# Low halves, a gate multiply and parts of the even mixer move from GpSimd to VectorE

## The chip, the cores and the metric

The kernel runs on one core of one Trainium2 chip. A core has five engines that each take their instructions in the order in which the program lists them: TensorE (PE in the profile, its weight loads PEld), VectorE (DVE), ScalarE (ACT), GpSimd (POOL) and SyncE (SP), which here only starts transfers between main memory and the core's own memories. The metric is the device time of one launch in microseconds, as the median of several runs.

## The reference, cut to what matters

One inference step of a small trunk with two layers. 128 context tokens and 512 latent tokens go through the same weights; the modulations (shift, scale, gate) come from a conditioning vector, one for the context and one for the latent tokens.

```python
for l in range(2):
    sh1, sc1, gt1, sh2, sc2, gt2 = ada_mod(c, w_ada[l], b_ada[l])
    h = rms_norm(x, g_mix_pre[l]) * (1 + sc1) + sh1
    y = even_mixer(h) if l == 0 else mla_mixer(h)   # each: h @ w_in ... @ w_out
    x = x + gt1 * rms_norm(y, g_mix_post[l])
    h = rms_norm(x, g_mlp_pre[l]) * (1 + sc2) + sh2
    y = square(relu(h @ w_mlp1[l])) @ w_mlp2[l]     # 1024 -> 4096 -> 1024
    x = x + gt2 * rms_norm(y, g_mlp_post[l])

# even_mixer: 4 heads of gated linear attention and 4 of retention, in both directions
#   o_gla = rms_norm(scan_f + scan_b, gla_norm) * silu(ga); o_ret = rms_norm(...) * silu(gb)
# mla_mixer: q, ckv, kpe = split(h @ w_in); 8 heads; keys and values from ckv @ w_kv_b
#   o = softmax(q k^T / sqrt(192)) v over 128 context, 128 cached and 512 latent keys
```

A context token attends to context tokens alone. All is float32.

## The kernel before

**Tiles and stages.** The 640 tokens are five tiles of 128 (t = 0 the context, 1 to 4 the latent tokens). The stages follow each other: the even mixer with its input projection, its output projection, the first MLP, the odd mixer (attention) with its input projection, its output projection, the second MLP. Beside them run the modulations of later stages (`rada`, `ada`), and all weights are loaded once, in the order of a list.

**Float32 by three products.** TensorE multiplies in a short format (fp32r). So each weight and each activation is kept as two halves, high = the cast, low = what the cast has lost, and `mm3` makes high x high, high x low and low x high. The cast is ScalarE's (`nc.scalar.copy`), the low half is a subtraction (`tensor_sub`), on GpSimd or VectorE by an argument `lo`. In the trace a weight's raw copy is `raw`, its halves are `wh` and `wl` (where both lie in one tile, `wp`), the activations' halves are `hT` (two constant tiles, the high one and the low one), and the float32 value ahead of it `h`.

**A weight's way.** `weights` (L409) starts a load as soon as one of three `raw` buffers is free; `weight_rooms` (L423) waits for the load and takes a place among ten `w` buffers; `weight_split` (L449) does the cast and the low half, gives `raw` back and announces the weight. `nat_units` (L462) does this for projections, in four parts of two contraction blocks each for each group of columns; the first group of the odd layer's projection is 256 wide (splits of 128x512), the second 320. `mlp_units` (L860) does it for the MLP in eight blocks: four weights of the first and four of the second product, each 128x1024. Before the change the low halves of both projections of each mixer, of the attention heads' weights, and of the first four weights of each MLP are GpSimd's; the other MLP weights are VectorE's.

**An activation's way.** `pre_norm` (L723) takes the square sum (ScalarE), a root by a few one-column instructions (`sm`), scales the tile (`y` or `xn`), has TensorE turn it in eight blocks (`ps`), modulates four of them on VectorE and four on ScalarE (`h`), and splits them (`hT`) in two halves of 128x512. Its low half is GpSimd's after the first tiles and after the MLP, and "either" after an output projection. The MLP's `tail` (L1033) runs for each token tile after the last block: it adds the last partial sum to `y` (VectorE), sums its squares (ScalarE), multiplies by the gate (GpSimd, L1046), then `residual` (L774) and the next `pre_norm`. The squared ReLU is `relu` (L1019): ScalarE's relu and square, GpSimd's square in float32, VectorE's difference.

**What sets the order.** The instructions are written by a list scheduler, `Weave` (L95). Each piece of work is a generator that hands instructions to engines and yields where the next one depends on the last. The planner keeps a clock for each engine, with a cost for each instruction from `Engine.way` (L267): VectorE 0.07 + n/960 us, GpSimd 0.2 + 0.00215 n, for n elements of a row. One more clock, "port", stands for the memory port that VectorE's two-input instructions and GpSimd's share. Among those that are ready at an engine's next free time it emits the one of the lowest priority number, on VectorE the one of the oldest thread, and so on. A weight's split has priority 1 (or 0 with `prio=0`), the token tiles' work 0 or below. With "either" the planner picks the engine that would end first. The result is one fixed list for each engine. At run time an engine takes its list in order, and an instruction whose input is not there holds up all behind it.

All instructions are issued from one line, `emit` (L269), so in the profile every row bears L269 and is known by its tiles. Here is the code that the change touches and what calls it.

## Time and profile before

| | |
|---|---|
| time, median of 3 runs | 1567.67 us (1564.66 to 1568.7) |
| profiled execution | 1567.55 us |
| its span in the trace | 1565.8 us |
| mean granted TensorE clock | 0.982 of full speed |
| read and written in main memory | 158.73 and 5.96 MB, 105 GB/s |

The span is what the trace covers; the profiled execution's time has 1.75 us more around it. The two-dimensional picture of the span (40 slices of 39 us, digits in tenths of busy time) shows how the engines share it:

```profile
PE   5999999999999999999998999989999999999997
DVE  4254755655777787777667688865675333334335
ACT  3583533645323223223245466654543222322322
POOL 1433744331012012102165110051202101211213
PEclk8999999999999999999997999999999999999999
```

GpSimd is busiest from 39 to 352 us (slices 2 to 9: the even mixer, its output projection and the first MLP's entry), from 783 to 861 us (slices 21 and 22: the odd layer's entry) and from 1018 to 1057 us (slice 27: the weights of the odd output projection). TensorE is below nine tenths in slices 1, 22, 27 and 40, and its granted clock below nine tenths in slices 1 and 22.

### The profile page before, as it was taken

How to read it: one execution, taken by the hardware profiler on the slowest of the kernel's cores; microseconds unless marked ns; L12 is line 12 of the kernel's file. 1: busy time of each engine (PE TensorE's matmuls, PEld its weight loads, DVE VectorE, ACT ScalarE, POOL GpSimd, SP SyncE). 2: the span in 40 equal slices, each digit the busy share in tenths (PEclk: the TensorE clock that was granted, in tenths of full speed). 3: DMA queues.
4: the chain of work that ended last, by engine and by line, in shares of the span. 5: the costliest groups of instructions: out<-in, count | busy, mean ns of one | idle time of the engine just before them, and what ended most of it. 6: DMA issues, size and time to landing. Idle time of an engine off the chain costs nothing.

```text
span 1565.8 us, 23013 instructions
## 1 busy us (share of the span) xinstructions
PE 1508.6 (96%) x8731; PEld 1338.3 (85%) x8731; DVE 939.7 (60%) x1776; ACT 635.0 (41%) x1467; POOL 387.3 (25%) x317
## 2 busy tenths in 40 slices
PE   5999999999999999999998999989999999999997
PEld 1687888888899889989977899978889988998996
DVE  4254755655777787777667688865675333334335
ACT  3583533645323223223245466654543222322322
POOL 1433744331012012102165110051202101211213
PEclk8999999999999999999997999999999999999999
DMA  9455322222554445444323001032353322222211
GB/s 333 150 180 182 87 73 62 93 85 92 182 159 139 140 139 146 142 133 128 99 85 120 14 21 28 28 97 72 102 173 103 88 76 74 81 72 67 77 54 67
DMA packets 146734, 166.19 MB, mean 106 GB/s; under 512 B 11984, under 2 KB 92480, under 8 KB 146624
## 3 DMA queue, kind: packets, MB, share of 16 engines
q1 hardware_dynamic: 146624, 164.73, 34.4%
q8 instruction: 68, 1.11, 0.3%
q14 instruction: 42, 0.34, 0.1%
HBM read 158.73 MB, written 5.96 MB: 105 GB/s over the span
## 4 chain that ended last, share of the span: by engine, by line
PE 89%; DVE 4%; ACT 3%; DMA 1%; issue 1%; POOL 1%; SPq 1%; DVEq 0%; ACTq 0%; POOLq 0%
PE p L269 56%; PE pg L269 18%; PE ps L269 12%; PE pqk L269 2%; DVE sm L269 1%; PE pv L269 1%; ACT junk L269 1%; DVE x L269 1%; DMA x<-in_x_sample 1%; DMA rada<-in_w_ada 1%; SPq L269 1%; DVE y L269 0%; DVE prob L269 0%; ACT h L269 0%; ACT wh L269 0%
## 5 line engine op out<-in xcount | busy, mean ns | idle before, releaser
L269 PE MATMUL p<-hT,wh 128*128 128x256 f32 (+1 forms) x2048 | 450.7, 311 | 4.8 <-ACT hT L269 4.2
L269 PE MATMUL p<-wh,hid 128*128 128x512 f32 x1280 | 398.7, 390 | 0.0
L269 PEld LDWEIGHTS p<-hT,wh 128*128 128x128 f32 x2048 | 347.4, 190 | 6.9 <-ACT hT L269 4.7
L269 PE MATMUL p<-hT,wl 128*128 128x256 f32 (+1 forms) x1024 | 317.8, 310 | 0.0
L269 POOL TENSOR_TENSOR r<-r 128x384 f32<-128x384 f32 (+1 forms) x128 | 132.6, 1036 | 729.5 <-ACT hid L269 700.5
L269 PEld LDWEIGHTS p<-wh,hid 128*128 128x128 f32 x1280 | 240.3, 188 | 49.6
L269 ACT CAST wh<-raw 128x1024 fp32r<-128x1024 f32 (+3 forms) x169 | 172.5, 1026 | 261.6 <-PE p L269 220.6
L269 PE MATMUL pg<-wh,hT 128*128 128x512 f32 (+3 forms) x840 | 265.6, 388 | 0.0
L269 PE MATMUL p<-wl,hid 128*128 128x512 f32 x640 | 249.6, 390 | 0.0
L269 DVE TENSOR_TENSOR wl<-raw,wh 128x1024 fp32r<-128x1024 f32 x121 | 148.1, 1224 | 107.5 <-ACT wh L269 107.3
L269 PEld LDWEIGHTS p<-hT,wl 128*128 128x128 f32 x1024 | 195.0, 190 | 0.0
L269 PEld LDWEIGHTS pg<-wh,hT 128*128 128x128 f32 x840 | 155.6, 191 | 29.4 <-issue 6.7
L269 ACT ACTIVATE r<-p 128x384 f32<-128x384 f32 (+1 forms) x128 | 56.1, 438 | 268.5 <-PE p L269 268.5
L269 DVE TENSOR_TENSOR y<-y,p 128x512 f32<-128x512 f32 x140 | 95.8, 685 | 103.5 <-PE p L269 103.2
L269 POOL TENSOR_TENSOR wl<-raw,wh 128x1024 fp32r<-128x1024 f32 (+3 forms) x44 | 100.1, 2290 | 217.5 <-ACT wh L269 106.8
L269 DVE SCALAR_TENSOR_TENSOR ada<-rada,cT,ada 128x512 f32<-128x512 f32 x196 | 146.8, 783 | 0.0
L269 DVE TENSOR_TENSOR hid<-r,hid 128x384 fp32r<-128x384 f32 (+1 forms) x128 | 63.6, 497 | 130.5 <-POOL r L269 130.5
L269 PE MATMUL pg<-wl,hT 128*128 128x512 f32 (+3 forms) x360 | 141.6, 393 | 0.0
L269 PEld LDWEIGHTS p<-wl,hid 128*128 128x128 f32 x640 | 120.2, 188 | 24.1
L269 PEld LDWEIGHTS pg<-wl,hT 128*128 128x128 f32 x360 | 68.6, 191 | 13.6 <-issue 4.4
L269 ACT ACTIVATE hid<-r 128x384 fp32r<-128x384 f32 (+1 forms) x128 | 60.4, 472 | 2.2
L269 POOL TENSOR_TENSOR wp<-raw,wp 128x512 fp32r<-128x512 f32 (+1 forms) x18 | 25.2, 1405 | 96.3 <-ACT wp L269 96.3
(257 smaller groups left out, 2006.2 us busy)
## 6 DMA issues: line engine op xcount, KB each, us to landing
raw<-in_w_mlp SPq DMA_DIRECT2D x128, 512.0 KB, 4.1
rada<-in_w_ada SPq DMA_DIRECT2D x160, 256.0 KB, 3.4
rada<-in_w_ada SPq DMA_DIRECT2D x16, 512.0 KB, 9.1
raw<-in_w_in_even SPq DMA_DIRECT2D x16, 512.0 KB, 3.8
x<-in_x_sample SPq DMA_DIRECT2D x8, 512.0 KB, 6.8
gate<-gate SPq DMA_DIRECT2D x8, 512.0 KB, 4.7
raw<-in_w_out_even SPq DMA_DIRECT2D x8, 512.0 KB, 3.7
raw<-in_w_out_odd SPq DMA_DIRECT2D x8, 512.0 KB, 3.8
```

The lines of the kernel that those rows point to most:

```text
L269: emit = lambda: real(*a, **k)
```

## The change

Every low half that GpSimd made becomes VectorE's: of the weights of both mixers' projections, of the attention heads, of the first block of each MLP, and of the activations (`hT`); after the output projections, where the planner chose, VectorE now makes it always. The MLP tail's multiply by the gate becomes VectorE's. In the even mixer three operations do: the sum of the two masked score halves (A + B), the gate's multiply by the norm's gain (ga), and the two decayed keys (`ks`). GpSimd keeps the squared ReLU, the fills, the backward states, its half of the rotation, and one state product of the context tile. The planner's costs are not changed; with other engines for these instructions it writes other lists.

```diff
--- before.py
+++ after.py
@@ -720,7 +720,7 @@
             self.drop(hp, hw)
 
 
-    def pre_norm(self, t, x, xn, sm, mods, ready, halves=None, lo="gpsimd"):
+    def pre_norm(self, t, x, xn, sm, mods, ready, halves=None):
 
 
         nc, w = self.nc, self.w
@@ -758,7 +758,7 @@
             k = slice(half * 4, half * 4 + 4)
             nc.scalar.copy(self.hT[0][:, t, k], h)
             yield
-            getattr(nc, lo).tensor_sub(self.hT[1][:, t, k], h, self.hT[0][:, t, k].bitcast(F32))
+            nc.vector.tensor_sub(self.hT[1][:, t, k], h, self.hT[0][:, t, k].bitcast(F32))
             self.drop(hh)
             w.set(evs[half])
             if halves:
@@ -828,16 +828,16 @@
 
         io = self.io
         self.wlist = []
-        self.u_in_even = self.nat_units(io["w_in_even"][0], EVEN_GROUPS, "gpsimd", prio=0)
+        self.u_in_even = self.nat_units(io["w_in_even"][0], EVEN_GROUPS, prio=0)
         self.loaded = Event()
         self.wlist.insert(2, self.loaded)
         self.even_rooms = [Event() for _ in range(4)]
-        self.u_out_even = (self.nat_units(io["w_out_even"][0], OUT_GROUPS[:1], "gpsimd")
-                           + self.nat_units(io["w_out_even"][0], OUT_GROUPS[1:], "gpsimd", rooms=self.even_rooms))
+        self.u_out_even = (self.nat_units(io["w_out_even"][0], OUT_GROUPS[:1])
+                           + self.nat_units(io["w_out_even"][0], OUT_GROUPS[1:], rooms=self.even_rooms))
         self.u_mlp = [self.mlp_units(0)]
         self.odd_rooms = [Event() for _ in range(4)]
-        self.u_in_odd = (self.nat_units(io["w_in_odd"][0], ODD_GROUPS[:1], "gpsimd", pair=True)
-                         + self.nat_units(io["w_in_odd"][0], ODD_GROUPS[1:], "gpsimd", rooms=self.odd_rooms))
+        self.u_in_odd = (self.nat_units(io["w_in_odd"][0], ODD_GROUPS[:1], pair=True)
+                         + self.nat_units(io["w_in_odd"][0], ODD_GROUPS[1:], rooms=self.odd_rooms))
         wq = io["w_q_b"][0].rearrange("(k p) (h c) -> p k h c", p=P, h=HC)
         wkv = io["w_kv_b"][0].rearrange("(k p) (h s c) -> p k h s c", p=P, h=HC, s=2)
         self.u_qpe = self.weight(lambda raw: [(raw[:, k], wq[:, k, :, 128:192]) for k in range(2)], [2, HC, 64])
@@ -846,15 +846,15 @@
         for h in range(HC):
             self.u_h.append(self.weight(lambda raw, h=h: [x for k in range(2) for x in (
                 (raw[:, k, 0], wq[:, k, h, 0:P]), (raw[:, k, 1], wkv[:, k, h, 0]))], [2, 2, P],
-                lo="gpsimd", pair=True, quota=quota))
+                pair=True, quota=quota))
             if h % 2 == 0:
                 self.u_v.append(self.weight(lambda raw, h=h: [(raw[:, k], wkv[:, k, h:h + 2, 1]) for k in range(2)],
-                                            [2, 2, P], lo="gpsimd", pair=True, quota=quota))
+                                            [2, 2, P], pair=True, quota=quota))
         self.heads_out = Event()
         self.wlist.append(self.heads_out)
         self.odd_out_rooms = [Event() for _ in range(4)]
-        self.u_out_odd = (self.nat_units(io["w_out_odd"][0], OUT_GROUPS[:1], "gpsimd")
-                          + self.nat_units(io["w_out_odd"][0], OUT_GROUPS[1:], "gpsimd", rooms=self.odd_out_rooms))
+        self.u_out_odd = (self.nat_units(io["w_out_odd"][0], OUT_GROUPS[:1])
+                          + self.nat_units(io["w_out_odd"][0], OUT_GROUPS[1:], rooms=self.odd_out_rooms))
         self.u_mlp.append(self.mlp_units(1))
 
     def mlp_units(self, l):
@@ -862,7 +862,7 @@
         w2 = self.io["w_mlp2"][l].rearrange("(f p) n -> p f n", p=P)
         res = []
         for b in range(FF // 512):
-            lo = "vector" if b else "gpsimd"
+            lo = "vector"
             prio = 0 if b else 1
             u1 = [self.weight(w1[:, :, fc * P:(fc + 1) * P], [KC, P], lo, prio=prio) for fc in range(b * 4, b * 4 + 4)]
             u2 = [[self.weight(w2[:, r0:r0 + 2, h * 512:h * 512 + 512], [2, 512], prio=prio)
@@ -978,7 +978,7 @@
             self.at_last(left, lambda: w.set(gfree))
             x = xs[t][0]
             yield from self.residual(x, y, sm)
-            yield from self.pre_norm(t, x, y, sm, mods, ready, None, "either")
+            yield from self.pre_norm(t, x, y, sm, mods, ready)
             self.drop(hy, hs)
 
         for t in range(NT):
@@ -1043,7 +1043,7 @@
                 yield
                 nc.scalar.activation(self.junk[:, 0:512], y[:, s], AF.Square, accum_out=sm[:, 4 + half:5 + half])
                 yield
-                nc.gpsimd.tensor_mul(y[:, s], y[:, s], gr[c][:, s])
+                nc.vector.tensor_mul(y[:, s], y[:, s], gr[c][:, s])
                 yield
             if gfree:
                 self.at_last(left, lambda: w.set(gfree))
@@ -1444,7 +1444,7 @@
                 nc.vector.copy_predicated(h4(M), masks[:, d].unsqueeze(1).broadcast_to((P, NH, P)), h4(pas[d][0]))
                 self.drop(pas[d][1])
                 yield
-            nc.gpsimd.tensor_add(A, A, B)
+            nc.vector.tensor_add(A, A, B)
             self.drop(hkt)
 
             v, hv = yield va
@@ -1459,7 +1459,7 @@
             ga, hga = yield from self.take(sg, [P, 512], F32, "ga")
             yield from silu_of(ps, hp, ga)
             yield
-            nc.gpsimd.tensor_mul(h4(ga), h4(ga), gn.unsqueeze(1).broadcast_to((P, NH, P)))
+            nc.vector.tensor_mul(h4(ga), h4(ga), gn.unsqueeze(1).broadcast_to((P, NH, P)))
             yield from mix_out(t, "gla", qt, v, pr, 1.0 / 64.0, 0.125, ga, ga)
             ya, hya = ga, hga
             self.drop(hqt, hv, hee)
@@ -1507,7 +1507,7 @@
             self.drop(hp)
             kv_ = k.rearrange("p (h c) -> p h c", h=NH)
             for d in range(2):
-                nc.gpsimd.tensor_mul(ks[:, :, d], kv_, kd[:, :, d].unsqueeze(2).broadcast_to((P, NH, 64)))
+                nc.vector.tensor_mul(ks[:, :, d], kv_, kd[:, :, d].unsqueeze(2).broadcast_to((P, NH, 64)))
             self.drop(hqk)
             yield
```

The numbers in the names below only count the tiles made, and differ between the two programs.

**The odd layer's entry.** Before, GpSimd's list stands as follows at the end of the first MLP. `y_3655` and `y_3657` are token tiles 3 and 4, `wp_7460` and `wp_7461` the third and fourth part of the projection's first weight group, `wp_7516` and the rest the second group.

```order
L269 TENSOR_TENSOR y_3655<-y_3655,gate_94 128x512
L269 TENSOR_TENSOR hT_92<-h_7420,hT_91 128x512
L269 TENSOR_TENSOR hT_92<-h_7422,hT_91 128x512
L269 TENSOR_TENSOR wp_7460<-raw_7221,wp_7460 128x512
L269 TENSOR_TENSOR wp_7461<-raw_7288,wp_7461 128x512
L269 TENSOR_TENSOR wp_7516<-raw_7300,wp_7516 128x640
L269 TENSOR_TENSOR y_3655<-y_3655,gate_94 128x512
L269 TENSOR_TENSOR y_3657<-y_3657,gate_94 128x512
L269 TENSOR_TENSOR hT_92<-h_7589,hT_91 128x512
L269 TENSOR_TENSOR hT_92<-h_7592,hT_91 128x512
L269 TENSOR_TENSOR wp_7553<-raw_7520,wp_7553 128x640
L269 TENSOR_TENSOR wh_7562<-raw_7554,wh_7561 128x640
```

The splits stand between the gate multiplies of tiles 3 and 4, and beside VectorE's own list. Now the same two parts are `wp_7478` and `wp_7479` in VectorE's list; `sm_3658` and `y_3657` belong to tile 4.

```order
L269 TENSOR_SCALAR sm_3658<-sm_3658 128x1
L269 TENSOR_SCALAR h_7649<-ps_7639,mod_4782,mod_4206 128x128 x2
L269 TENSOR_TENSOR wp_7478<-raw_7221,wp_7478 128x512
L269 SCALAR_TENSOR_TENSOR sm_3658<-sm_3658 128x1
L269 TENSOR_TENSOR hT_92<-h_7651,hT_91 128x512
L269 TENSOR_SCALAR sm_3658<-sm_3658 128x1
L269 TENSOR_TENSOR hT_92<-h_7649,hT_91 128x512
L269 TENSOR_TENSOR sm_3658<-sm_3658 128x1
L269 TENSOR_SCALAR y_3657<-x_3205,sm_3658 128x1024
L269 TENSOR_TENSOR wp_7479<-raw_7283,wp_7479 128x512
L269 TENSOR_SCALAR h_7696<-ps_7686,mod_4782,mod_4206 128x128 x4
```

The last addition of the MLP (the last partial sum onto tile 4) is 28 rows ahead of `wp_7478` and 35 ahead of `wp_7479`. So the two splits moved behind the gate multiplies, residuals and normalisations of the tiles before. On TensorE the first projection group of the first tile (`pg`) before runs through its four weight parts at once:

```order
L269 MATMUL pg_7525<-wp_7266,hT_91 128x256 x2
L269 MATMUL pg_7525<-wp_7266,hT_92 128x256
L269 MATMUL pg_7525<-wp_7460,hT_91 128x256 x2
L269 MATMUL pg_7525<-wp_7460,hT_92 128x256
L269 MATMUL pg_7525<-wp_7460,hT_91 128x256 x2
L269 MATMUL pg_7525<-wp_7460,hT_92 128x256
L269 MATMUL pg_7525<-wp_7461,hT_91 128x256 x2
L269 MATMUL pg_7525<-wp_7461,hT_92 128x256
L269 MATMUL pg_7525<-wp_7461,hT_91 128x256 x2
L269 MATMUL pg_7525<-wp_7461,hT_92 128x256
L269 MATMUL pg_7526<-wp_7516,hT_91 128x320 x2
```

Now the eight turns of tile 4 (`ps` with the identity) are put between the third part's products and the fourth's, which begin in the last two rows:

```order
L269 MATMUL pg_7562<-wp_7478,hT_91 128x256 x2
L269 MATMUL pg_7562<-wp_7478,hT_92 128x256
L269 MATMUL ps_7686<-ident,y_3657 128x128
L269 MATMUL ps_7687<-ident,y_3657 128x128
L269 MATMUL ps_7686<-ident,y_3657 128x128
L269 MATMUL ps_7687<-ident,y_3657 128x128
L269 MATMUL ps_7686<-ident,y_3657 128x128
L269 MATMUL ps_7687<-ident,y_3657 128x128
L269 MATMUL ps_7686<-ident,y_3657 128x128
L269 MATMUL ps_7687<-ident,y_3657 128x128
L269 MATMUL pg_7562<-wp_7479,hT_91 128x256 x2
L269 MATMUL pg_7562<-wp_7479,hT_92 128x256
```

What moved: the third part's products stand ahead of the turns of tile 4, the fourth part's behind them, and 241 TensorE instructions of this stage follow `wp_7479`'s.

**From softmax to the output projection.** VectorE before, at the last head's softmax: `prob` are the probabilities of a tile, `sm` their sums, `pt` the turned probabilities, each `sm` with its own number a tile.

```order
L269 TENSOR_TENSOR sm_10367<-sm_10367 128x1
L269 TENSOR_TENSOR sm_10399<-sm_10399 128x1
L269 RECIPROCAL sm_10367<-sm_10367 128x1
L269 TENSOR_TENSOR hT_92<-ps_10383,hT_91 128x128
L269 TENSOR_SCALAR prob_10366<-prob_10366,sm_10367 128x640
L269 RECIPROCAL sm_10399<-sm_10399 128x1
L269 TENSOR_TENSOR hT_92<-ps_10457,hT_91 128x2x128
L269 TENSOR_SCALAR prob_10398<-prob_10398,sm_10399 128x640
```

Between them GpSimd made the output projection's splits at the same time. VectorE now, at the same place:

```order
L269 TENSOR_SCALAR sm_10378<-sm_10378 128x1
L269 TENSOR_TENSOR wl_10261<-raw_9827,wh_10260 128x1024
L269 TENSOR_TENSOR wl_10419<-raw_10331,wh_10418 128x1024
L269 TENSOR_TENSOR sm_10378<-sm_10378 128x1
L269 RECIPROCAL sm_10378<-sm_10378 128x1
L269 TENSOR_SCALAR prob_10377<-prob_10377,sm_10378 128x640
L269 TENSOR_TENSOR wh_10421<-raw_10409,wh_10420 128x1024
L269 TENSOR_TENSOR pt_8256<-ps_10496,pt_8255 128x512
```

What moved: two splits (`wl`) stand between a tile's sum and its scaling of the probabilities, and a third behind the scaling.

## The prediction

> **What bounds the kernel now.** I read the page's busy line and chain first, then the windows, and last the timeline of the few stretches where TensorE waits.
>
> ```profile
> PE 1508.6 (96%) x8731; PEld 1338.3 (85%) x8731; DVE 939.7 (60%) x1776; ACT 635.0 (41%) x1467; POOL 387.3 (25%) x317
> PE 89%; DVE 4%; ACT 3%; DMA 1%; issue 1%; POOL 1%; SPq 1%; DVEq 0%; ACTq 0%; POOLq 0%
> ```
>
> TensorE (PE) is busy 1508.6 of 1565.8 us and makes 89% of the chain that ended last. GpSimd (POOL) has 387.3 us of work, but 1% of the chain. Relieving an engine that is 25% busy is worth nothing by itself; the change can win or lose only inside the 57 us (1565.8 - 1508.6) in which PE stands still, and in the slow clock that follows such pauses. The windows say where they lie:
>
> ```profile
> 20.00:30.00 10.00, 6.18 (x30) 2.76 (x28) 4.56 (x14) 5.36 (x11) 2.21 (x1) 0.69 1.05 394
> 30.00:40.00 10.00, 7.84 (x34) 3.95 (x31) 7.97 (x17) 4.50 (x9) 5.92 (x5) 0.63 1.05 391
> 200.00:300.00 100.00, 99.55 (x547) 83.46 (x546) 57.58 (x114) 44.10 (x81) 43.26 (x35) 1.00 0.18 54
> 820.00:830.00 10.00, 6.93 (x32) 6.56 (x32) 8.07 (x14) 5.74 (x18) 9.33 (x7) 0.66 0.36 110
> 840.00:850.00 10.00, 6.01 (x27) 5.12 (x26) 9.10 (x32) 6.04 (x17) 3.69 (x4) 0.51 0.24 87
> 900.00:1000.00 100.00, 98.32 (x737) 96.49 (x735) 81.73 (x251) 68.17 (x218) 9.88 (x8) 1.00 0.10 30
> 1030.00:1040.00 10.00, 6.25 (x39) 5.52 (x37) 6.90 (x19) 5.79 (x18) 3.68 (x2) 0.87 0.46 141
> ```
>
> Columns are the window, its length, busy us of PE, PEld, DVE, ACT, POOL, then granted clock, DMA share and GB/s. Between the pauses PE is full (99.55 of 100 us), so moving work there changes nothing unless the new owner falls behind. In the pauses VectorE (DVE) is the busy engine (9.10 of 10 us at 840), and the clock drops to 0.51 to 0.69. At first sight it is a bad moment to give DVE more work.
>
> **Why DVE looks fuller than it is.** Its rows while POOL works, and the same rows while POOL rests:
>
> ```profile
> 345.69 4.75 POOL L269 TENSOR_TENSOR wl<-raw,wh 128x1024 fp32r<-128x1024 f32 x2
> 345.98 2.12 DVE L269 TENSOR_TENSOR sm<-sm 128x1 f32<-128x1 f32 x1
> 348.20 3.33 DVE L269 SCALAR_TENSOR_TENSOR x<-y,sm,x 128x1024 f32<-128x1024 f32 x1
> 357.40 1.28 DVE L269 SCALAR_TENSOR_TENSOR x<-y,sm,x 128x1024 f32<-128x1024 f32 x1
> 1557.02 0.21 DVE L269 SCALAR_TENSOR_TENSOR sm<-sm 128x1 f32<-128x1 f32 x1
> 1557.46 0.16 DVE L269 TENSOR_TENSOR sm<-sm 128x1 f32<-128x1 f32 x1
> ```
>
> An instruction on one column takes 0.16 us alone and 2.12 us inside a GpSimd split; the residual takes 1.28 and 3.33. DVE is not computing for that long, it is held until GpSimd's instruction ends. So a part of DVE's busy time is waiting for POOL, and goes away with POOL's work.
>
> **What each moved instruction costs.**
>
> ```profile
> L269 POOL TENSOR_TENSOR wl<-raw,wh 128x1024 fp32r<-128x1024 f32 x32 | 79.5, 2506 | 166.5 <-ACT wh L269 86.2 <-DVE sm L269 34.6 <-PE ps L269 20.4
> L269 DVE TENSOR_TENSOR wl<-raw,wh 128x1024 fp32r<-128x1024 f32 x121 | 148.1, 1224 | 107.5 <-ACT wh L269 107.3
> L269 POOL TENSOR_TENSOR hT<-h,hT 128x512 fp32r<-128x512 f32 x20 | 27.8, 1403 | 12.2 <-ACT hT L269 11.1 <-DMA dist<-in_consts 1.1
> L269 DVE TENSOR_TENSOR hT<-h,hT 128x512 fp32r<-128x512 f32 x20 | 13.1, 689 | 3.9 <-ACT hT L269 3.8
> L269 DVE SCALAR_TENSOR_TENSOR sm<-sm 128x1 f32<-128x1 f32 x50 | 25.8, 524 | 13.0 <-ACT sm L269 13.0
> L269 DVE TENSOR_TENSOR sm<-sm 128x1 f32<-128x1 f32 x82 | 22.4, 279 | 5.8 <-ACT prob L269 4.4
> L269 DVE TENSOR_SCALAR h<-ps,mod,mod 128x128 f32<-128x128 f32 x80 | 28.8, 404 | 15.6 <-PE ps L269 15.2 <-POOL hT L269 0.2
> ```
>
> The same split takes 2506 ns on POOL and 1224 on DVE (ratio 0.49), the 512-wide form 1403 and 689. The gate multiply is of that 512-wide, two-input form, so I take 0.69 for it too. What stays on POOL is the squared ReLU, the fills, the backward states and half of the rotation, about 164 us; 223 move and become 0.49 x 223 = 110 us on DVE. Returned are at least 50 x (0.524 - 0.21) = 16 us and 82 x (0.279 - 0.16) = 10 us of holds on the statistics alone. DVE should end near 1010 us (65%), so in the mean it still has room. The sum goes place by place; negative is faster.
>
> **1. The start (20 to 40 us).**
>
> ```profile
> 24.97 2.21 POOL L269 TENSOR_TENSOR wl<-raw,wh 128x960 fp32r<-128x960 f32 x1 [24.53 <-DMA rada<-in_w_ada]
> 25.32 1.87 DVE L269 SCALAR_TENSOR_TENSOR sm<-sm 128x1 f32<-128x1 f32 x1
> 30.49 1.82 DVE L269 TENSOR_TENSOR sm<-sm 128x1 f32<-128x1 f32 x1
> 61.92 4.74 DMA rada<-in_w_ada
> ```
>
> The statistics of the second and third token tile are held for 1.87 - 0.21 and 1.82 - 0.16, 3.3 us on the path to the first projection. Now DVE makes the first split itself, ahead of that statistic (about 1.1 us, from 1.224 for a slightly wider one), and the second one behind the normalised tile, where it delays nothing. Left are about 2.2 us, and 0.7 from the activation's low half (1.40 to 0.69). A transfer stands in the chain at 61.92, so part may be hidden there. I take **-2.5**; ends 0 (the DMA ends it anyway) and -6 (all of PE's 6.0 idle us in these windows).
>
> **2. The two MLP entries (350 and 1100 us).** The splits of an MLP's first block hold the statistics and residual of token tile 2 by 2.12 - 0.16 and 3.33 - 1.28 us, and the first MLP matmuls wait for that tile:
>
> ```profile
> 361.04 0.45 PE L269 MATMUL p<-hT,wh 128*128 128x384 f32 x1 [2.10 <-ACT hT L269]
> ```
>
> 4.0 us of holds go; of the four splits (1.224 each) now on DVE three stand between this tile's instructions, but where DVE waited for ScalarE or PE anyway. I take **-2.5** for each entry, the wait and a little clock, **-5** together; ends +1 and -8 (a split that waits for its cast pushes the tile back, or both entries lose every wait).
>
> **3. The odd layer's entry (803 to 869 us): the place that decides.**
>
> ```profile
> 802.04 0.67 DVE L269 TENSOR_TENSOR y<-y,p 128x512 f32<-128x512 f32 x1
> 803.01 0.75 DVE L269 TENSOR_SCALAR y<-x,sm 128x1024 f32<-128x1024 f32 x1
> 812.46 5.47 POOL L269 TENSOR_TENSOR wp<-raw,wp 128x512 fp32r<-128x512 f32 x3
> 813.51:869.36 55.85, 45.21 (x297) 43.07 (x296) 39.56 (x113) 31.12 (x100) 28.46 (x22) 0.85 0.37 112
> 845.71:869.36 23.65, 23.65 (x169) 23.55 (x168) 14.23 (x52) 12.13 (x43) 6.81 (x7) 0.91 0.15 57
> ```
>
> PE ends the MLP at 813.5 and needs until 869.4 for 297 instructions, 10.6 us of it idle. In the new order DVE works through all five tiles first. The third and fourth low half of the projection's first weight group (wp_7478, wp_7479) stand 28 and 35 rows behind the last MLP addition, and PE's order puts 241 instructions behind wp_7479. From the second half of tile 2's addition (802.04 before) to the last addition the order holds some 12.6 us of free-running DVE work, so DVE gets there about when PE delivers, 814.5. From there to wp_7479 stand: fifteen small statistics (2.5 us), ten 512-wide passes with both splits (6.9), two residuals (2.6), three normalisations (0.75 each, 2.25), eight h pieces (0.40 each, the group of 80 above, 3.2) and an estimated 0.7 for two evictions: 18 us, less some 2.5 because consecutive instructions overlap. With 1.5 us for waits on ScalarE wp_7479 ends at 831.5. PE then has 241 instructions at 23.65 / 169 = 0.140 us: 33.7 us, end 865.2 against 869.4. I take **-3**; ends -8 (no waits, full clock) and +8 (DVE needs ten more us for the tiles). It breaks even if wp_7479 ends at 835.5.
>
> On the clock after such a pause, by the Trainium skill, page TensorE: Matmul & The Clock Gate, section What's actually happening, about 3.4 us without work halves the clock until about 3.4 us of work have passed. The windows at 820 and 840 agree with the direction (0.66, 0.51). By that rule one long wait before wp_7479 would cost an estimated 1.7 us more, and this term would be -1.3 instead of -3.
>
> **4. Attention (870 to 1020 us).** Twelve 512-wide splits move, 12 x 0.69 = 8.3 us onto a DVE that is 82% busy beside a PE at 98% (window at 900); the holds that go are of the same size. I take **0**, covered by DVE's spare 18%; without that cover the price is up to +5, and below nothing -2.
>
> **5. From softmax to the output projection (1030 to 1050 us).**
>
> ```profile
> 1033.34 0.54 DVE L269 TENSOR_SCALAR prob<-prob,sm 128x640 f32<-128x640 f32 x1
> 1035.14 2.34 POOL L269 TENSOR_TENSOR wl<-raw,wh 128x1024 fp32r<-128x1024 f32 x1 [3.79 <-ACT wh L269]
> 1035.30 2.53 DVE L269 TENSOR_SCALAR prob<-prob,sm 128x640 f32<-128x640 f32 x1
> 1037.97 1.94 PE L269 MATMUL ps<-ident,prob 128*128 128x128 f32 x8 [3.54 <-DVE sm L269]
> 1044.32 2.39 DVE L269 TENSOR_SCALAR prob<-prob,sm 128x640 f32<-128x640 f32 x1
> 1047.03 2.29 DVE L269 TENSOR_SCALAR prob<-prob,sm 128x640 f32<-128x640 f32 x1
> ```
>
> Scaling the probabilities takes 0.54 us free and 2.53, 2.39 and 2.29 beside a split: 5.6 us of holds in the last head's softmax, and PE waits 3.54 us behind the first. DVE now makes these splits; two stand ahead of the last tile's scaling (2.4 us). I take 5.6 - 2.4 = 3.2, and a little clock: **-3.5**; ends 0 and -6.
>
> **6. The end.**
>
> ```profile
> 1557.94 1.65 POOL L269 TENSOR_TENSOR y<-y,gate 128x512 f32<-128x512 f32 x1 [1.37 <-ACT junk L269]
> 1560.07 0.20 DVE L269 TENSOR_SCALAR sm<-sm 128x1 f32<-128x1 f32 x1
> ```
>
> The last gate multiply ends at 1559.6; on DVE it takes 0.69 from about 1557.8, and the statistic at 1560.07 can follow at 1558.55: **-1.5**; ends -1 and -2.
>
> **The even mixer** (weight splits, ga, qt, kr between 100 and 330 us) I cost at nothing: PE is full there by the window at 200 and DVE 58% busy. If DVE became the later one, every us is a us; I keep ends of 0 and +3. On SyncE's queue only constants, cache and parking transfers change places; earlier splits free the three raw buffers earlier, so no load moves behind its need.
>
> **Sum:** -2.5 - 5 - 3 + 0 - 3.5 - 1.5 = -15.5. The profiled execution took 1567.55 us, 0.1 below the median of 1567.67, so the forecast is **1552 us**.
>
> **Rivals.**
>
> *DVE becomes the bound at the odd entry (slower).* The splits are queued behind five tiles of residual and normalisation, where POOL made them beside DVE at 812.46. If the tiles take as long as now and wp_7479 comes only at an estimated 851, some 5 us past the 845.71 from which PE now runs unbroken, PE ends at 851 + 33.7 = 884.7, +15.3 instead of -3. If DVE is then the later engine in the attention stage too (+5), the total is 1552 + 18.3 + 5 = 1575. It turns slower than before once wp_7479 ends later than about 848. For it speaks DVE's 9.10 of 10 us at 840; against it, that much of this is held time.
>
> *Nothing net: 1566.* The waits of PE are refilled by others (the DMA at 61.92, ScalarE's casts, DVE's own splits), and only the end's 1.5 us stay. By the Trainium skill, page Perfetto Trace Analysis, section Optimizing Scalar/DVE Operations, moving operations between these two engines might not help, since they share a read port. That would be this rival, with the sum at 1566. The rows speak against it, since the same split holds the port 2.5 us from POOL and 1.2 from DVE.
>
> *Half: 1560.* The odd entry breaks even or loses 1 to 2 us, and the holds come back in part as DVE's own splits.
>
> *More: 1543.* The odd entry, the start and the entries reach their far ends, with the clock staying up.
>
> **How the numbers follow.** A measurement can tell about 0.3% (4.7 us) from no change. Forecast (1548 to 1557) 0.44, half 0.20, more 0.12, nothing net 0.13, slower 0.11. Faster by over 0.3% (below 1563): 0.44 + 0.20 + 0.12 = 0.76, less 0.02 of the half case that falls short of it, is 0.74. Same: 0.13, those 0.02 and 0.01 of the slower case, 0.16. Slower: the other 0.10. The range takes the forecast, the half case and most of the further gain, up to where nothing is left of it: 1542 to 1566.
>
> **What would show it.** POOL near 164 us, DVE near 1010; the statistics' two groups near 0.21 and 0.16 us each; no scaling of probabilities above 0.8 us; PE's idle time near 45 us or less; PE's wait at the odd entry as one block before wp_7479, ending by 833. Wrong would be a DVE row that waits for a cast with statistics behind it, idle time of PE in the even stage, or wp_7479 after 836.

## The result, and the profile after

The changed kernel takes 1542.75 us (median of 4 runs, 1541.48 to 1544.89) against 1567.95 us (1564.66 to 1568.7, 4 runs). The ratio is 0.9845, 95% interval 0.9827 to 0.9863: 25 us less, where 15.5 were forecast; the time lies 0.75 us above the lower end of the predicted range of 1542 to 1566. The profiled execution took 1542.66 us, its span is 1540.9.

From the page of the changed kernel, the busy line and the chain by engines:

```profile
PE 1495.1 (97%) x8731; PEld 1329.5 (86%) x8731; DVE 962.6 (62%) x1912; ACT 636.6 (41%) x1467; POOL 165.4 (11%) x181
PE 91%; DVE 4%; ACT 2%; DMA 2%; issue 1%; SPq 0%; DVEq 0%; ACTq 0%
```

TensorE's idle time (span less busy time) fell by 11.4 us, from 57.2 to 45.8, about the 45 that the prediction named. The larger part of the gain, 13.5 us, is shorter busy time (1508.6 to 1495.1): the traces record 57.2 us at half clock before and 39.8 after, and these 17.4 us less explain up to 8.7 of it. The rest is open.

GpSimd fell from 387.3 to 165.4 us. VectorE took over 222 us of its work and grew by only 22.9. The groups show why:

```profile
L269 DVE TENSOR_TENSOR wl<-raw,wh 128x1024 fp32r<-128x1024 f32 x153 | 186.8, 1223 | 122.9 <-ACT wh L269 122.6
L269 DVE TENSOR_SCALAR prob<-prob,sm 128x640 f32<-128x640 f32 x32 | 17.5, 547 | 0.3
L269 DVE TENSOR_TENSOR sm<-sm 128x1 f32<-128x1 f32 x82 | 13.0, 159 | 5.0 <-ACT prob L269 3.3
L269 DVE SCALAR_TENSOR_TENSOR sm<-sm 128x1 f32<-128x1 f32 x50 | 10.6, 215 | 6.2 <-ACT sm L269 6.2
```

The two groups of statistics fell from 279 to 159 ns and from 524 to 215. The scaling of the probabilities takes 547 ns in the mean, and the longest of the 32 takes 554.

The windows of the changed kernel (columns as in the prediction) at the first MLP's entry, the odd entry, and the end of attention:

```profile
350.00:360.00 10.00, 10.00 (x51) 8.61 (x50) 7.81 (x17) 6.43 (x17) 0.00 (x0) 1.00 0.58 191
360.00:370.00 10.00, 10.00 (x63) 9.92 (x62) 7.79 (x22) 6.15 (x17) 1.78 (x2) 1.00 0.34 124
810.00:820.00 10.00, 3.58 (x21) 3.07 (x20) 9.63 (x26) 6.37 (x20) 0.00 (x0) 0.75 0.50 157
820.00:830.00 10.00, 6.29 (x33) 5.99 (x34) 6.70 (x18) 5.75 (x17) 0.00 (x0) 0.57 0.40 118
1020.00:1030.00 10.00, 10.00 (x62) 8.73 (x61) 9.51 (x21) 6.11 (x17) 0.00 (x0) 1.00 0.35 106
```

At the MLP's entry TensorE no longer stands still, and between the last scores and the output projection it waits 1.1 us in all, where it waited 5.3; its clock stays at 1 at both places. At the odd entry it still does: 10.1 us of idle time in these two windows, at a clock of 0.75 and 0.57.

To see where the 25 us come from, I took the start of the same TensorE product in both traces at six points: late in the even layer's output projection, early in the first MLP, the first and the last scores of the attention, late in the odd output projection, early in the second MLP. The difference between neighbouring points is the gain of the stretch between them (spans, us, negative is faster):

| stretch | forecast | measured |
|---|---|---|
| start and even stage | -2.5 | -1.1 |
| first MLP's entry | -2.5 | -4.9 |
| odd entry, up to the first scores | -3 | -4.7 |
| attention | 0 | -1.5 |
| softmax to output projection | -3.5 | -6.9 |
| second MLP's entry | -2.5 | -4.8 |
| end | -1.5 | -1.1 |
| sum | -15.5 | -24.9 |

Inside both MLPs the distance stays the same to 0.1 us.

### The profile page after: what moved, and what is told of

It is laid out like the page before. It is cut to its first block, busy times and chain, and to the rows that moved or that the text cites. A ratio compares the mean times of both kernels' runs of the same rounds, so it can differ in the third digit from the quotient of the medians.

```text
span 1540.9 us, 22938 instructions
## 1 busy us (share of the span) xinstructions
PE 1495.1 (97%) x8731; PEld 1329.5 (86%) x8731; DVE 962.6 (62%) x1912; ACT 636.6 (41%) x1467; POOL 165.4 (11%) x181
## 4 chain that ended last, share of the span: by engine, by line
PE 91%; DVE 4%; ACT 2%; DMA 2%; issue 1%; SPq 0%; DVEq 0%; ACTq 0%
PE p L269 56%; PE pg L269 19%; PE ps L269 13%; PE pqk L269 2%; DMA rada<-in_w_ada 1%; PE pv L269 1%; DVE y L269 1%; DVE sm L269 1%; ACT junk L269 1%; DVE x L269 1%; DMA raw<-in_w_in_even 0%; ACT h L269 0%; DVE rope L269 0%; ACT sm L269 0%; PE pc L269 0%
## 5 line engine op out<-in xcount | busy, mean ns | idle before, releaser
L269 DVE TENSOR_TENSOR wl<-raw,wh 128x1024 fp32r<-128x1024 f32 (+3 forms) x165 | 197.3, 1199 | 132.9 <-ACT wh L269 128.0
L269 PE MATMUL ps<-kn,qn 128*128 128x320 f32 (+1 forms) x216 | 47.8, 311 | 0.9 <-DVE hT L269 0.4
L269 PE MATMUL ps<-pt,v 128*128 128x256 f32 (+1 forms) x264 | 43.5, 290 | 1.1 <-DVE pt L269 0.7
```

The lines of the kernel that those rows point to most:

```text
L269: emit = lambda: real(*a, **k)
```

## The experiments

The theory: GpSimd's two-input instructions hold VectorE, and the gain comes where they did so on TensorE's path. Its rivals: the planner's new order carries the gain; GpSimd's splits only came late; the moved work itself costs or brings nothing.

**Half of the change each.** e1 takes the changed `plan` and `mlp_units` alone, e2 all the rest alone.

> Only the weights' low halves go to VectorE; the activations' low halves, the gate multiply and the even mixer's three operations stay on GpSimd. Theory (GpSimd's two-input instructions hold VectorE at the MLP entries, the softmax and the start): the weights' splits are the long ones and stand at those places, so about 17 of the 25 us come: -5 at each MLP entry, -6.5 from softmax to output projection, -1 at the start; near 1551 us. Rival (the new order of the odd entry and the shorter tails of tiles carry the gain): under 10 us, 1558 or more.

> Only the activations' low halves, the gate multiply and the even mixer's three operations go to VectorE; the weights' low halves stay on GpSimd. Theory: the end's 1.1 us and a part of the odd entry, 2 to 6 us in all, near 1564 us, with the waits of 2.1 us at both MLP entries and of 3.5 us behind the last head's softmax still there. Rival: 15 us or more.

e1: 1549.37 us, ratio 0.9884 (0.987 to 0.9899). e2: 1563.08, ratio 0.9968 (0.9955 to 0.9981). By stretch, beside the whole change:

| stretch | whole | e1 weights | e2 others |
|---|---|---|---|
| start and even stage | -1.1 | +1.9 | -0.4 |
| first MLP's entry | -4.9 | -4.8 | -0.4 |
| odd entry | -4.7 | 0.0 | -8.1 |
| attention | -1.5 | -1.0 | +1.9 |
| softmax to output projection | -6.9 | -6.8 | 0.0 |
| second MLP's entry | -4.8 | -4.8 | +1.1 |
| end | -1.1 | 0.0 | -1.1 |

(e1's profiled execution, 1552.15 us, was the longest of its four, so its stretches sum to 15.4 and not to the 18 of the medians; e2's, 1560.52 us, was the shortest of its five, so its stretches sum to 7.0 and not to 4.2.) In their totals both met the theory; e1's start lost 1.9 us where 1 was expected to come. The entries and the softmax are the weights' alone: e2 still waits 2.10 us at both MLP entries and 3.05 behind the last softmax (2.10 and 3.54 in the kernel before). The end is the gate multiply's alone. The odd entry was not expected so: there the other parts gain 8.1, the weights nothing, and both together less than the others alone.

**GpSimd beside VectorE, with nobody waiting for it.** e3 and e4 add work on GpSimd beside sixteen splits, the eight of the odd output projection and the first four of each MLP, where `a` is half of the cast weight:

```diff
+            for s in (slice(0, 256), slice(256, 512)):
+                g.tensor_sub(self.spare, a[:, s].rearrange("p (j q) -> p j q", q=P), ident)   # e3
+            g.tensor_copy(self.spare[:, 0, 0:1], a[:, 0:1])                                     # e4
+            for _ in range(4):
+                g.memset(self.spare, 0.0)
```

> The changed kernel, and beside each split of the odd output projection and of the first four weights of each MLP GpSimd makes four subtractions 128x256 of its own (the cast weight less a constant, into a tile that nobody reads). The lists of the other engines are the same. Theory (holds): VectorE is held again at these places, so 8 to 17 of the 16.6 us that they gained are lost, 1551 to 1559 us, with statistics of 128x1 near 1 us and scalings of the probabilities of 128x640 over 1 us there. Rival (the splits on GpSimd came late, and VectorE's own order is better): nobody waits for these subtractions, 0 us, 1543.

> As e3_dummy_sub, but in place of each pair of subtractions GpSimd copies one column and then fills a tile 128x256 four times, which reads nothing. Theory (VectorE is held by two-input work of GpSimd, not by GpSimd being busy): within 1 us of the changed kernel, 1543. If it costs as much as the subtractions, any work of GpSimd holds VectorE.

e3: 1556.21 us, 13.5 more than the changed kernel (ratio to the kernel before 0.9927, 0.9912 to 0.9942). e4: 1543.48, 0.7 more (0.9846, 0.983 to 0.9863). Timeline of e3 at the first MLP's entry (start, duration, engine, instruction):

```profile
342.48 10.99 POOL L483 TENSOR_TENSOR spare<-wh,ident 128x256 bf16<-128x256 f32 x9
342.64 0.59 DVE L269 TENSOR_TENSOR sm<-sm 128x1 f32<-128x1 f32 x1
343.32 1.79 DVE L269 SCALAR_TENSOR_TENSOR x<-y,sm,x 128x1024 f32<-128x1024 f32 x1
345.03 3.44 DVE L269 TENSOR_TENSOR wl<-raw,wh 128x1024 fp32r<-128x1024 f32 x2
349.91 1.30 DVE L269 TENSOR_SCALAR y<-x,sm 128x1024 f32<-128x1024 f32 x1
351.26 0.44 PE L269 MATMUL ps<-ident,y 128*128 128x128 f32 x2 [3.08 <-DVE y L269]
```

No other engine reads `spare`, and the other engines' lists are those of the changed kernel. Still the residual takes 1.79 instead of 1.28 us, the normalisation 1.30 instead of 0.75, and TensorE waits 3.08 us for the tile. By stretch e3 lost all of the 4.9 and 4.8 us of the two entries, but only 2.6 of 6.9 after the softmax. Fills at the same place cost nothing measurable, though GpSimd is busy for 54.8 us with them and their one-column copies, and for 65.9 us with e3's subtractions. So it is not GpSimd being busy that holds VectorE, it is what the subtractions do and the fills do not: they read whole tiles. Whether a GpSimd instruction with one input would hold it as well, no run here shows.

**The engine alone, in the same order.** e9 makes those sixteen splits on GpSimd, but plans them as VectorE's, so that the lists of the other engines keep their order:

```diff
-            eng.tensor_sub(b, r, a.bitcast(F32))
+            e, us, _, port = eng.way("tensor_sub", (b, r, a.bitcast(F32)), {})
+            self.w.put((e, us, lambda a=a, b=b, r=r: self.tc.nc.gpsimd.tensor_sub(b, r, a.bitcast(F32)), port))
```

> The changed kernel, but the low halves of the odd output projection and of the first four weights of each MLP are made by GpSimd, at the place and with the planner's cost that they have on VectorE, so that the lists of the other engines keep their order. Theory (it is the engine: GpSimd holds VectorE, and its split takes 2.5 us): 12 to 17 of the 16.6 us at these three places are lost, 1555 to 1560 us, and scalings of the probabilities of 128x640 over 2 us come back. Rival (the planner's new order carries the gain there): under 5 us lost, 1548 or less. The small subtractions beside VectorE's splits gave back 5 at each MLP entry and only 2.6 from softmax to output projection; this run says whether the rest of that place is the engine's or the order's.

e9: 1560.34 us, 17.6 more than the changed kernel and 0.3 above the expected range; ratio to the kernel before 0.9958 (0.9945 to 0.9972). Timeline at the first MLP's entry:

```profile
343.02 7.13 POOL L460 TENSOR_TENSOR wl<-raw,wh 128x1024 fp32r<-128x1024 f32 x3 [68.76 <-ACT sm L269]
343.25 2.19 DVE L269 SCALAR_TENSOR_TENSOR sm<-sm 128x1 f32<-128x1 f32 x1 [0.84 <-ACT sm L269]
345.67 2.13 DVE L269 TENSOR_TENSOR sm<-sm 128x1 f32<-128x1 f32 x1
347.89 3.33 DVE L269 SCALAR_TENSOR_TENSOR x<-y,sm,x 128x1024 f32<-128x1024 f32 x1
355.20 0.69 PE L269 MATMUL ps<-ident,y 128*128 128x128 f32 x2 [4.69 <-DVE y L269]
```

The holds of the kernel before are back to the hundredth (3.33 us for the residual). The entries lose 6.9 and 7.0 us against the changed kernel, 2 more than they had gained: it may be that the order of before had put some of TensorE's work into that wait, which no run separates. After the softmax 3.2 of 6.9 us are lost, though one scaling takes 2.20 us again. So at the entries the engine is the whole of the gain, since in an unchanged order its return loses all of it; after the softmax the engine is about half. The other half (3.7 us) may lie in the new order or in the attention heads' splits; these two were not separated.

**The slow clock.** e5 fills the pause ahead of each MLP in the kernel before:

```diff
+                if b == f == g == 0:
+                    w.later(lambda: [self.tc.nc.tensor.matmul(ps[:, :P], self.ident, self.ident, start=True, stop=True)
+                                     for _ in range(10)])
```

> The kernel before, with ten small matmuls (identity by identity, into the bank that the first real product then clears) ahead of the first product of each MLP, where TensorE waits 2.1 us for the last token tile. They fit into the wait. Theory (each such pause is paid twice, once as the pause and once as the slow clock behind it): the granted clock stays at 1 at both entries, the pause stays, and 2 us come at each, -4 in all, near 1563.5 us; the entries' 4.9 us of gain in the changed kernel are then 2.7 of pause and 2.1 of clock. Rival (the slow clock costs nothing there): 0.

e5: 1565.24 us beside 1567.13, ratio 0.9991 (0.9982 to 1.0). The same ten microseconds in the windows of the kernel before and of e5:

```profile
359.00:369.00 10.00, 7.67 (x37) 7.34 (x38) 7.58 (x21) 6.08 (x19) 0.00 (x0) 0.83 0.35 119
```

```profile
359.00:369.00 10.00, 9.16 (x62) 8.49 (x60) 8.01 (x22) 6.79 (x20) 0.00 (x0) 1.00 0.35 126
```

The filling took 2.4 us, 0.3 more than the pause. The clock stays at 1, but each entry gains only 0.7 us, not the 2 expected. Behind the filled pause stand two waits. The first was there before, the second is new (first the kernel before, then e5):

```profile
361.77 0.69 PE L269 MATMUL p<-hT,wh 128*128 128x384 f32 x1 [0.28 <-DVE hT L269]
```

```profile
362.06 0.45 PE L269 MATMUL p<-hT,wh 128*128 128x384 f32 x1 [0.29 <-DVE hT L269]
364.98 0.44 PE L269 MATMUL ps<-ident,y 128*128 128x128 f32 x2 [0.55 <-DVE y L269]
```

This expectation was wrong. The 3.4 us at half clock are worth 1.7 us; 0.3 of that went into the longer filling and 0.55 into a wait for VectorE's next tile that the slow clock had covered, which leaves about 0.8. In the whole time the difference is not clear of noise (the interval ends at 1.0). With VectorE freed, in the changed kernel, TensorE's busy time at the two entries is 2.2 and 2.0 us shorter.

**The odd entry.** e6 (and once more as e12) puts the splits of the first weight group ahead in VectorE's list, e7 gives the odd projection's splits back to GpSimd:

```diff
-        self.u_in_odd = (self.nat_units(io["w_in_odd"][0], ODD_GROUPS[:1], pair=True)
+        self.u_in_odd = (self.nat_units(io["w_in_odd"][0], ODD_GROUPS[:1], pair=True, prio=0)   # e6, e12
+        self.u_in_odd = (self.nat_units(io["w_in_odd"][0], ODD_GROUPS[:1], "gpsimd", pair=True)  # e7, both groups
```

> The changed kernel, with the splits of the odd projection's first weight group at the priority of the tiles' work, so that the third and fourth part are split at the MLP's last additions and not 28 and 35 rows behind them. Theory (at the odd entry the order of the splits in VectorE's list is what costs): TensorE has the projection of tiles 0 to 2 to do in the waits; 5 to 10 us come, near 1536 us. Rival (VectorE's sum of work sets the entry): within 2 us of 1543.

> The changed kernel, with the low halves of the odd projection's weights back on GpSimd. With the weights on GpSimd everywhere and the rest on VectorE the odd entry gained 8.0 us, with the weights on VectorE and the rest on GpSimd 0.1, with both 4.7. Theory (moving the projection's splits behind the tiles loses there, moving the rest gains): -3.3 us against the changed kernel, near 1539.5. Rival (the holds weigh as much as the place in the list): 0 or slower.

> The kernel of e6_odd_in_first once more, on the same chip and beside e10 and e11, so that these are compared with it and not with a run on another day. Both theories: within 1.5 us of 1538.

e6: 1538.05 us (ratio 0.982, 0.9805 to 0.9835), e12: 1535.08 (0.9802, 0.9788 to 0.9815), e7: 1537.2 (0.9813, 0.9797 to 0.9829). e12 missed its expectation: the same kernel as e6, on another chip, came out 3 us lower, so medians from different chips compare no closer than that here. The stretches are the firmer measure. The odd entry gains 9.3 (e6), 9.2 (e12) and 8.6 us (e7) against the kernel before, where the change gained 4.7. First TensorE at the odd entry of the changed kernel, then of e12:

```profile
812.37 1.06 PE L269 MATMUL ps<-ident,y 128*128 128x128 f32 x8 [2.37 <-DVE y L269]
817.57 1.97 PE L269 MATMUL ps<-ident,y 128*128 128x128 f32 x8 [3.80 <-DVE y L269]
821.81 0.68 DVE L269 TENSOR_TENSOR wp<-raw,wp 128x512 fp32r<-128x512 f32 x1
822.54 1.44 PE L269 MATMUL pg<-wp,hT 128*128 128x256 f32 x5 [2.79 <-DVE wp L269]
824.34 0.75 DVE L269 TENSOR_SCALAR y<-x,sm 128x1024 f32<-128x1024 f32 x1
825.01 0.69 DVE L269 TENSOR_TENSOR wp<-raw,wp 128x512 fp32r<-128x512 f32 x1
825.15 1.97 PE L269 MATMUL ps<-ident,y 128*128 128x128 f32 x8 [1.17 <-DVE y L269]
826.77 5.45 PE L269 MATMUL pg<-wp,hT 128*128 128x256 f32 x35
```

```profile
807.77 0.68 DVE L269 TENSOR_TENSOR wp<-raw,wp 128x512 fp32r<-128x512 f32 x1
813.33 1.10 PE L269 MATMUL ps<-ident,y 128*128 128x128 f32 x8 [2.19 <-DVE y L269]
814.58 0.68 DVE L269 TENSOR_TENSOR wp<-raw,wp 128x512 fp32r<-128x512 f32 x1
815.32 0.58 PE L269 MATMUL pg<-wp,hT 128*128 128x256 f32 x1 [0.77 <-DVE wp L269]
```

With the last two splits at 807.77 and 814.58 instead of 821.81 and 825.01, TensorE has products of the projection to do while VectorE prepares the later tiles, and 10.1 us of waits become 3.0 (and 1.8 in small ones later in the stage). So the change's cost at this place was the splits' place in the list (e6's edit sets only their priority; the planner then also places some casts and products of this stage otherwise). VectorE's sum of work is the same in e6, 960.1 us beside 962.6.

**The even mixer's three operations.** e8 puts them back on GpSimd in the changed kernel, e11 in e6.

> The changed kernel, with the even mixer's three operations (A + B, ga, the decayed keys) back on GpSimd. Theory (TensorE is full there, and the operations are beside the path): within 1.5 us of 1543, no TensorE pause that the changed kernel lacks. Rival (they hold VectorE as the splits do): +3 or more, with pauses between 100 and 330 us.

> The kernel of e6_odd_in_first with the even mixer's three operations (A + B, ga, the decayed keys) back on GpSimd. With e8_even_pool the even stage ended 2.7 us earlier than in the changed kernel, but kernels with the same lists up to there differed by 1.6 among themselves. Theory (these operations are worth nothing either way, the difference is the start's): within 1.5 us of e6. Rival (GpSimd is the better place for them): 2 us or more under e6.

e8: 1541.37 us (0.9843, 0.9829 to 0.9858) beside 1542.75; e11: 1534.21 beside e12's 1535.08. Both are within 1.5 us, as the theory said. In their traces the even stage ends 3.7 and 3.1 us ahead of the kernel before, and in the nine other kernels with these operations on VectorE from 0.9 us behind it to 2.7 ahead. That would point to GpSimd as the better place, but e1, which has them on GpSimd too, ends the stage 1.9 us behind: nothing follows from it.

**Filling the pause at the odd entry.** e10 puts seven small products ahead of the first turn of tile 2 in e6's kernel.

> The kernel of e6_odd_in_first with seven small matmuls (identity by identity, 1.7 us) in the pause of 2.2 us that TensorE makes before it turns token tile 2 at the odd entry. At the MLP entries of the kernel before such filling kept the clock up and brought only 0.7 us each, as new waits stood right behind. Here 8 us of full work follow the pause. Theory (the slow clock costs its half where TensorE has work behind the pause): the 6.8 us at half clock go, 2 to 3.4 us come, near 1535.5. Rival (VectorE's tiles set the entry in any case): within 0.7 us of e6.

e10: 1536.35 us (1533.16 to 1537.36) beside e12's 1535.08 (1534.52 to 1537.88): no difference in the medians. By stretch its odd entry gains 11.3 us against e12's 9.2, so in these two executions the clock is worth the 2.1 us expected at that place, which the medians of the whole time do not show. e11 has the clock at 1 there without any filling. The windows behind the pause, of e12 and of e11:

```profile
815.00:821.50 6.50, 6.18 (x28) 5.89 (x29) 5.90 (x19) 4.58 (x16) 0.00 (x0) 0.51 0.97 312
```

```profile
812.40:818.90 6.50, 6.17 (x51) 6.00 (x52) 6.47 (x22) 5.32 (x20) 0.00 (x0) 1.00 1.00 316
```

In the same 6.5 us TensorE does 28 products in e12 and 51 in e11, after the same pause (2.19 and 2.18 us). e11's odd entry gains 11.6 us.

The best version is e11, 1534.21 us: ratio to the kernel before 0.9794 (0.9781 to 0.9807). e12 and e10 (0.9802, 0.9789 to 0.9816) can't be told from it; in the medians all three are faster than the changed kernel by 6 to 9 us, beside the 3 us by which one kernel differed between chips.

## Why the prediction was right, and where it was too small

**The number** lies nearer to the rival "More: 1543" (chance 0.12) than to the forecast of 1552 (chance 0.44 for 1548 to 1557), and it came by other terms than that rival named: the start gave 1.1 us and the odd entry 4.7, both far from their ends, while the MLP entries and the last softmax went beyond theirs. That the range held it by 0.75 us is in part luck.

**The mechanism** was right. "DVE is not computing for that long, it is held until GpSimd's instruction ends": e3 and e9 bring the holds back with the other engines' lists unchanged, e4 shows that a GpSimd busy with fills does not. The rival that nothing stays (1566) is refuted by 25 us. By the Trainium skill (page Perfetto Trace Analysis, section Optimizing Scalar/DVE Operations) moving work between these two engines might not help; here it did, by these 25 us. POOL (164 forecast, 165.4), the statistics (0.21 and 0.16 us forecast, 0.215 and 0.159) and the scalings came as forecast. DVE was forecast at 1010 and is at 962.6. The terms shown there give 939.7 + 110 - 26 = 1024, so 1010 already had 14 us without a row; measured, 87 us came back (939.7 + 110 - 962.6), since the residuals, scalings and splits were held too. One sign of being wrong did appear: at 342.15 us a VectorE split waits 0.51 us for its cast with tile 2's statistics behind it, and cost TensorE nothing there.

**The MLP entries** are the term that was mis-sized: -5 forecast, -9.7 measured, beyond the far end of -8. I took "the wait and a little clock", 2.1 + 0.4, with three splits in the way. Freed, the chain of tile 2 from its root to its normalised tile shrinks from 13.9 us (343.62 to 357.49 before) to 6.2 (343.30 to 349.49 after). Its first and last row before, then after:

```profile
343.62 2.14 DVE L269 SCALAR_TENSOR_TENSOR sm<-sm 128x1 f32<-128x1 f32 x1 [0.91 <-ACT sm L269]
356.74 0.75 DVE L269 TENSOR_SCALAR y<-x,sm 128x1024 f32<-128x1024 f32 x1
```

```profile
343.30 0.21 DVE L269 SCALAR_TENSOR_TENSOR sm<-sm 128x1 f32<-128x1 f32 x1
348.74 0.75 DVE L269 TENSOR_SCALAR y<-x,sm 128x1024 f32<-128x1024 f32 x1
```

That is 7.7 us, more than TensorE's wait, so all of its idle time in the two stretches went (2.6 and 2.7 us, small waits included), and its busy time fell by 2.2 and 2.0, of which the 3.4 us at half clock are 1.7.

**From softmax to the output projection** -3.5 was forecast and -6.9 measured, beyond the end of -6. I had charged two splits, 2.4 us, as standing ahead of the last scaling. They stand there, but TensorE had other work: its longest wait at this place is now 0.72 us:

```profile
1025.41 2.35 DVE L269 TENSOR_TENSOR wl<-raw,wh 128x1024 fp32r<-128x1024 f32 x2
1028.07 0.55 DVE L269 TENSOR_SCALAR prob<-prob,sm 128x640 f32<-128x640 f32 x1
1033.64 0.86 PE L269 MATMUL ps<-pt,v 128*128 128x256 f32 x5 [0.72 <-DVE pt L269]
```

The clock of 0.87 before is 1.00 now. Of the 6.9 us, 4.2 are idle time and 2.6 busy time: 6.8 us at half clock went with the waits. So the waits gave 1.0 more than the 3.2 us taken for them, and the larger part of what the sum missed lies in the clock, for which it had 0.3; at the MLP entries it had 0.4 each, where busy time fell by 2.2 and 2.0.

**The odd entry** came out at the time forecast, but not by the wait forecast. wp_7479 (split from 825.01) was forecast to end at 831.5; it ended at 825.70, and the MLP ahead was 5.9 us earlier, which makes 831.6. The stage then gained 4.7, where I took 3 and the working gave 4.2. But TensorE does not wait for wp_7479 in one block: three of its four waits are for normalised tiles (2.37, 3.80 and 1.17 us), one is for the third part, wp_7478 (2.79), and wp_7479's products follow the turns of tile 4 at 826.77 without a wait. Tile 4's normalisation (to 825.09) and wp_7479 ended within 0.7 us of each other, so that the stage's time fitted is in part luck. The rival (DVE the bound there) has its mechanism right: TensorE waits for VectorE's tiles and split, and e6 and e7 show that 4 to 5 us were lost by queueing the splits behind the tiles. Only its price did not reach the point where it turns the sum.

**The start** gave 1.1 instead of 2.5, **attention** 1.5 instead of 0, **the end** 1.1 instead of 1.5, all inside their ends. The start's gain can't be told from nothing: four kernels with the same lists up to there, the changed one among them, gain from 0.3 to 2.7 us.

On the clock, the Trainium skill's figure (page TensorE: Matmul & The Clock Gate, section What's actually happening: about 3.4 us without work) is longer than what the traces show: pauses of 2.10 and 2.19 us were enough (the last section has what decides).

## What to carry to other kernels

Where a small VectorE instruction takes 2 us, look at what GpSimd reads at that moment: an engine that is 25% busy can hold the one that everybody waits for, and moving its work cost half of its time here and gave the holds back. Add up what a held chain loses in all its instructions, and compare that with TensorE's wait: at the MLP entries the loss was larger, and the wait went whole. The slow clock behind it then went too, which brought nearly as much again; filling the wait alone brought less, where another wait lay behind it. After the move, put what the next stage needs first ahead in the new queue: that was worth another 4.5 us at the odd entry here.

## What the runs showed of the hardware that was not expected

The stretches at half clock are whole multiples of 3.41 us and begin on a fixed grid in each execution (the one that the program's end cuts off excepted). In the kernel before, three of them are 6.83, 10.24 and 3.41 us long and begin at 822.45, 839.52 and 887.31 us, 5 and 14 times 3.41 apart.

What decides is how busy TensorE is between two points of this grid. In the 14 profiles, of 70 full-clock stretches of 3.41 us in which TensorE was busy under 0.45 of the time, 69 were followed by half clock; of ten between 0.45 and 0.5 three were, of 66 between 0.5 and 0.8 one, and of the nearly 6000 above that two. The way back asks for more: none of 70 half-clock stretches with less than 0.8 was followed by full clock, and all 49 with 0.95 or more were.

So the same pause of 2.2 us is followed by 6.8 us at half clock in e12 and by none in e11, which gained 2.4 us more at that stage. In e12 the pause lies whole in one stretch (811.08 to 814.50, busy 0.36), in e11 a point of the grid at 810.02 divides it (busy 0.57 and 0.56). A pair of short waits does the same: 0.62 and 1.10 us in one stretch (busy 0.50) were followed by 3.4 us at half clock in e1, 0.62 and 1.09 us in two stretches (0.82 and 0.68) by none in the changed kernel.

GpSimd's fills (median 312 ns for 128x256) beside VectorE cost nothing measurable (e4: 0.7 us more in the median, within the spread of both kernels), its subtractions of the same size (median 778 ns) 5 us at each of two places.
